# Column sums of the adaLN modulation: transposes and a VectorE reduction in place of products with ones, and a first group on one accumulator

## The chip, the cores and the metric

One core of a Trainium2 chip runs the kernel. The metric is device time in microseconds (us), lower is better; each time is that of one execution, and the time of a kernel is the median of its runs. One further execution is recorded by the hardware profiler, and all rows of the profile come from it.

## The reference

The reference is one decoder layer in f32 with T = 256 positions, D = 2048 channels and a feed-forward width of 5632. What matters here is the modulation: a vector c of 2048 numbers is multiplied by a matrix of 2048 x 12288, and the product's six segments shift and scale the two normalised inputs and gate the two sub-layers.

```python
mod = jax.nn.silu(c) @ w_ada[l] + b_ada[l]
shift1, scale1, gate1, shift2, scale2, gate2 = jnp.split(mod[:, None, :], N_MOD, axis=-1)
h = rms_norm(x, norm1_gain[l]) * (1 + scale1) + shift1
x = x + gate1 * mixing_sublayer(h, w_in[l], ...)
h = rms_norm(x, norm2_gain[l]) * (1 + scale2) + shift2
x = x + gate2 * swiglu(h, w_ffn_in[l], w_ffn_out[l])
```

The mixing sub-layer projects h by w_in (the combined in-projection), runs three token mixers (stick-breaking, dilated and gated linear attention), gates their outputs, adds them and projects by w_out.

## The kernel before, in words

**Products.** Every large product is made of three TensorE (PE) matmuls on operands that are split into a high and a low half. A weight tile is loaded by SyncE's DMA queue into `raw` (line 149, four buffers), ScalarE casts it to the high half `whi` (L163), VectorE (DVE) subtracts that from `raw` to get the low half `wlo` (L164), and then PE runs high x high (L171), low weight x high h (L172) and high weight x low h (L173), each 128x512. A buffer of `raw` comes free when the low half has been taken from it, so a load is issued on SP when DVE gets there.

**The modulation.** w_ada is not multiplied on PE. Each 128-row chunk of its columns is loaded (L335 for the stream, the `load` function for the first group), and DVE multiplies it by the matching 128 numbers of silu(c) and adds it into an accumulator (`ada_mac`, L296 and L298; tiles `ada` and `AR`). After sixteen chunks an accumulator holds 128 partial sums per column, one in each partition. They are added by PE: a product whose stationary operand is 128 columns of the accumulator and whose moving operand is one column of ones (`column_sum`, L355) gives the 128 sums as one column of PSUM. `finish_columns` adds the bias (L369) and, for a scale, forms (1 + scale) * gain (L372). `make_h` then writes the high half of h on ScalarE (L482), the f32 value on ScalarE (L488) or, in the first group, on DVE (L486), and the low half on DVE (L489).

**Order of the work.** The sixteen 128-row chunks of h and w_in are contracted in five groups, `GROUPS` = (0,2), (2,5), (5,8), (8,11), (11,16), each over sixteen column blocks of 512 (`proj_block`), whose sums are kept in SBUF between groups. Shift and scale of group 0 are made ahead of everything (`first_group`): there are fillers of PE called `keep_warm` (L470, products whose result is not used, in batches of 22, 13 and 14), the normalised input x transposed by PE (L462), the macs of 16 chunks in two accumulators (even and odd chunks), then 2 x 4 products with ones, where the sums over the even and the odd accumulator are accumulated in PSUM. Shift and scale of group g + 1 are made while group g is multiplied (`ada_stream`): groups 1 to 3 in one piece each, with three column sums for shift and three for scale, and group 4 in two pieces of five sums. `turn_piece` issues the sums three stream steps after the last mac (`ADA_LATE`), behind the latest matmul, and the finish at raised priority. Shift and scale of the second norm (`columns`, tiles `mod2`) are made in the background of later work, sixteen sums for each in four steps, with a finish behind each step.

The order on each engine is settled when the kernel is built, by the order of the program's text, by the priorities (`prio`) and by `issue_after`, which puts an instruction behind a named one. Each engine then runs its queue in order. In the profile six column sums are twelve rows of L355: an f32 product with ones appears as two rows.

## Time and profile before

| | before |
|---|---|
| runs | 1588.58, 1589.65, 1590.91 us |
| median | 1589.65 us |
| profiled execution | 1589.52 us, its span 1587.7 us |
| mean granted PE clock | 0.999 |
| PE busy | 1574.7 us, 99% of the span |
| DVE busy | 1329.8 us, 84% |
| ScalarE (ACT) busy | 932.4 us, 59% |
| DMA | 402.28 MB, mean 253 GB/s |

A timeline row reads: start in us, duration in us, engine, line, operation, output <- input, partitions x elements, and count, where equal neighbours are drawn together in one row; a bracket at the end tells how long the engine was idle before it and what ended that. Rows of a matmul overlap, so PE's pace is read from the distance of starts. `PEld` is the weight load of a matmul, which overlaps the matmul before it. In a table of windows the columns are the stretch, its length, the busy time and row count of PE, PEld, DVE, ACT and POOL, the granted PE clock (1.00 is full), the share of DMA and GB/s.

### The profile page before, as it was taken

The numbers are of one execution on the slowest core, as the hardware profiler recorded it, in microseconds if no ns is written. First come the engines' busy times: TensorE is split into PE (matmuls) and PEld (weight loads), VectorE is DVE, ScalarE is ACT, GpSimd is POOL, SyncE is SP. The second block draws the span as 40 slices with busy tenths as digits, with TensorE's granted clock in tenths as the row PEclk, the third lists the DMA queues.
The fourth block names the chain that finished last, engine by engine and source line by source line (L and its number), as shares of the span: only waits on it lengthen the run. The fifth ranks groups of instructions, "written<-read, shape, count | busy, mean of one in ns | idle before, by whom it ended". The sixth has DMA issues, their size and how long they took to land.

```text
span 1587.7 us, 20515 instructions
## 1 busy us (share of the span) xinstructions
PE 1574.7 (99%) x7263; PEld 1304.5 (82%) x7263; DVE 1329.8 (84%) x1628; ACT 932.4 (59%) x1355; POOL 12.3 (1%) x24
## 2 busy tenths in 40 slices
PE   8999999999999999999999999999999999999999
PEld 7888878888888888788888888888888888888887
DVE  6788876589897877879677887999999999999996
ACT  5777867987665463544444644555555555455553
POOL 1000000000000000000000000000000000000000
PEclk9999999999999999999999999999999999999999
DMA  9899989667788799899687786666666666976664
GB/s 333 302 331 301 318 300 307 209 212 236 222 306 280 252 326 318 296 323 327 228 273 235 266 296 208 212 195 195 202 204 201 198 199 208 307 239 192 219 210 150
DMA packets 196878, 402.28 MB, mean 253 GB/s; under 512 B 13662, under 2 KB 32772, under 8 KB 196776
## 3 DMA queue, kind: packets, MB, share of 16 engines
q1 hardware_dynamic: 195512, 397.75, 75.9%
q0 software_dynamic: 1088, 3.16, 0.6%
q8 instruction: 57, 0.93, 0.2%
q14 instruction: 45, 0.37, 0.1%
q10 hardware_dynamic: 176, 0.07, 0.0%
HBM read 395.68 MB, written 5.24 MB: 253 GB/s over the span
## 4 chain that ended last, share of the span: by engine, by line
PE 85%; DVE 5%; DMA 5%; ACT 3%; issue 2%; SPq 0%; DVEq 0%; ACTq 0%
PE acc L173 21%; PE acc L172 21%; PE acc L171 21%; PE misc L171 6%; PE misc L172 6%; PE misc L173 6%; DVE wlo L164 1%; DMA raw<-w_in 1%; ACT whi L163 1%; DVE wlo L1356 1%; PE misc L355 1%; DMA OS<-w_ada 1%; PE misc L832 1%; DMA raw<-w_ffn_in 1%; DMA OD<-w_ada 1%
## 5 line engine op out<-in xcount | busy, mean ns | idle before, releaser
L164 DVE TENSOR_TENSOR wlo<-raw,whi 128x1024 fp32r<-128x1024 f32 (+1 forms) x344 | 383.4, 1123 | 140.6 <-ACT whi L163 139.2
L163 ACT CAST whi<-raw 128x1024 fp32r<-128x1024 f32 (+1 forms) x344 | 332.9, 972 | 271.3 <-PE acc L173 163.1
L171 PE MATMUL acc<-whi,H 128*128 128x512 f32 x1145 | 449.1, 393 | 0.6 <-ACT whi L1370 0.3
L172 PE MATMUL acc<-wlo,H 128*128 128x512 f32 x1145 | 447.7, 391 | 0.6 <-DVE wlo L164 0.6
L173 PE MATMUL acc<-whi,H 128*128 128x512 f32 x1145 | 446.6, 391 | 0.6 <-DVE H L489 0.5
L172 PEld LDWEIGHTS acc<-wlo,H 128*128 128x128 f32 x1145 | 215.5, 188 | 46.5 <-DVE wlo L164 2.7
L173 PEld LDWEIGHTS acc<-whi,H 128*128 128x128 f32 x1145 | 215.2, 188 | 46.2 <-DVE H L489 1.3
L171 PEld LDWEIGHTS acc<-whi,H 128*128 128x128 f32 x1145 | 215.5, 188 | 44.6 <-ACT whi L1370 0.8
L1370 ACT CAST whi<-raw 128x1024 fp32r<-128x1024 f32 (+1 forms) x163 | 155.3, 968 | 110.7 <-PE acc L173 35.3
L1356 DVE TENSOR_TENSOR wlo<-raw,whi 128x1024 fp32r<-128x1024 f32 (+1 forms) x163 | 178.0, 1115 | 10.6 <-ACT whi L1370 9.5
L173 PE MATMUL acc<-whi,A 128*128 128x512 f32 x234 | 91.1, 389 | 0.0
L172 PE MATMUL acc<-wlo,A 128*128 128x512 f32 x224 | 87.4, 390 | 1.4 <-DVE wlo L164 1.4
L529 ACT COPY A<-acc 128x512 f32<-128x512 f32 x129 | 73.1, 584 | 25.9 <-PE acc L173 24.4
L171 PE MATMUL acc<-whi,A 128*128 128x512 f32 x224 | 87.4, 391 | 0.0
L171 PE MATMUL misc<-whi,H 128*128 128x512 f32 (+1 forms) x201 | 78.3, 389 | 0.2 <-DVE misc L1406 0.2
L172 PE MATMUL misc<-wlo,H 128*128 128x512 f32 (+1 forms) x201 | 78.0, 388 | 0.0
L173 PE MATMUL misc<-whi,H 128*128 128x512 f32 (+1 forms) x201 | 77.9, 387 | 0.0
L1370 ACT CAST A<-raw 128x1024 fp32r<-128x1024 f32 (+1 forms) x47 | 46.0, 988 | 34.4 <-PE acc L173 14.3
L1356 DVE TENSOR_TENSOR A<-raw,A 128x1024 fp32r<-128x1024 f32 (+2 forms) x59 | 61.3, 1050 | 5.5 <-ACT A L1370 5.0
L519 ACT COPY acc<-A 128x512 f32<-128x512 f32 x97 | 55.8, 597 | 3.8 <-DVE A L531 3.5
L298 DVE SCALAR_TENSOR_TENSOR ada<-AR,csil,ada 128x1024 f32<-128x1024 f32 x39 | 49.7, 1281 | 2.7 <-DMA AR<-w_ada 2.7
L173 PEld LDWEIGHTS acc<-whi,A 128*128 128x128 f32 x234 | 43.9, 188 | 9.1
(500 smaller groups left out, 2512.1 us busy)
## 6 DMA issues: line engine op xcount, KB each, us to landing
raw<-w_in SPq DMA_DIRECT2D x186, 512.0 KB, 4.9
raw<-w_ffn_in SPq DMA_DIRECT2D x176, 512.0 KB, 4.5
raw<-w_ffn_out SPq DMA_DIRECT2D x74, 512.0 KB, 5.1
AR<-w_ada SPq DMA_DIRECT2D x58, 512.0 KB, 5.0
raw<-w_in SPq DMA_DIRECT2D x64, 256.0 KB, 4.5
raw<-w_out SPq DMA_DIRECT2D x32, 512.0 KB, 5.0
KC<-w_ada SPq DMA_DIRECT2D x23, 512.0 KB, 5.9
KD<-w_ada SPq DMA_DIRECT2D x19, 512.0 KB, 5.9
```

What stands on the lines that cost most here:

```text
L163: state["cast"] = nc.scalar.copy(hi[:, :n, :], raw[:, :n, :])
L164: state["split"] = nc.vector.tensor_tensor(lo[:, :n, :], raw[:, :n, :], hi[:, :n, :].bitcast(F32), op=ALU.subtract)
L171: nc.tensor.matmul(ps, lh, rh, start=start, stop=False, skip_group_check=seeded)
L172: nc.tensor.matmul(ps, lh, rl, start=False, stop=False, skip_group_check=seeded)
L173: state["mm"] = nc.tensor.matmul(ps, ll, rh, start=False, stop=stop, skip_group_check=seeded)
L298: nc.vector.scalar_tensor_tensor(acc, raw, c, acc, op0=ALU.mult, op1=ALU.add)
L355: return nc.tensor.matmul(ps, acc, ones[:, 0:1], start=start, stop=stop)
L519: nc.scalar.copy(pss[t], A[b][:, t, :])
L529: nc.scalar.copy(A[b][:, t, :], pss[t])
L832: nc.tensor.matmul(ps[:n, t * N_GLA + h, :].rearrange("p (s l) -> p s l", l=L), at(f, h, t)[:, :n], odd(at(f, h, t)), start=True, stop=True,)
L1356: done = nc.vector.tensor_tensor(dst, x, y, op=ALU.subtract)
L1370: nc.scalar.copy(hi[:, :n, :], src)
```

## The change

There are three edits.

1. *First group.* One accumulator takes all sixteen macs, so each of the four sums is one product with ones. The third batch of fillers has seven matmuls for fourteen, and a new batch of two stands between the two pairs of sums. The first weight load is written out here; the low half of its two 128x512 parts is made in two instructions (in the new file L599), the first behind the last mac, the second behind the low half of h of chunk 0. Before, it was one instruction ahead of the last two macs.
2. *Stream and second norm.* `turned_sums` takes the place of the products with ones: for each 128 columns one PE transpose (with the identity as the moving operand) into a bank of PSUM, [128, n, 128], and then one DVE `reduce_sum` over the last axis for all n. In `turn_piece` n is 3, or 5 in two parts of 3 and 2; the reduction runs at raised priority and writes a small tile that the finish reads.
3. *Second norm.* For each segment there are four times four transposes and a reduction, and one finish over all sixteen columns behind them in place of four.

```diff
--- before.py
+++ after.py
@@ -37,7 +37,7 @@
 LOOK = 3
 DEFER = 4
 AHEAD = 4000
-WARM = (22, 13, 14)
+WARM = (22, 13, 7, 2)
 GROUPED = 16
 GROUPS = ((0, 2), (2, 5), (5, 8), (8, 11), (11, 16))
 ADA_BY = (16, 37, 58, 80)
@@ -289,13 +289,13 @@
 
     w_ada = I["w_ada"]
 
-    def ada_mac(acc, raw, k, zero=True, fresh=False):
+    def ada_mac(acc, raw, k, zero=True):
 
         c = csil[:, k : k + 1]
-        if k == 0 and zero or fresh:
-            nc.vector.tensor_scalar(acc, raw, c, None, op0=ALU.mult)
+        if k == 0 and zero:
+            return nc.vector.tensor_scalar(acc, raw, c, None, op0=ALU.mult)
         else:
-            nc.vector.scalar_tensor_tensor(acc, raw, c, acc, op0=ALU.mult, op1=ALU.add)
+            return nc.vector.scalar_tensor_tensor(acc, raw, c, acc, op0=ALU.mult, op1=ALU.add)
 
     ADA_TAGS = ("T4", "T5", "OS0", "OS1", "OS2", "OD")
     ADA_LATE = 3
@@ -347,20 +347,25 @@
     def turn_piece(g, js, acc, n):
         finish = mod_columns(g)
         for i, j in enumerate(js):
-            ps = column_sums(acc[:, i, :], n, state["mm"].ins)
+            sums = small([P, n])
+            half = (n + 1) // 2 if n > 4 else n
+            for a in range(0, n, half):
+                turned_sums(sums[:, a : min(n, a + half)], acc[:, i, a * P : min(n, a + half) * P], state["mm"].ins, True)
             with prio():
-                finish(j, ps)
-
-    def column_sum(ps, acc, start, stop):
-        return nc.tensor.matmul(ps, acc, ones[:, 0:1], start=start, stop=stop)
-
-    def column_sums(acc, n, behind):
-
-        ps = misc_bank([P, n])
+                finish(j, sums)
+
+    def column_sum(ps, acc):
+        return nc.tensor.matmul(ps, acc, ones[:, 0:1], start=True, stop=True)
+
+    def turned_sums(dst, acc, behind=None, soon=False):
+
+        n = dst.shape[1]
+        ps = misc_bank([P, n, P])
         for i in range(n):
-            with tc.issue_after(behind):
-                column_sum(ps[:, i : i + 1], acc[:, i * P : (i + 1) * P], True, True)
-        return ps
+            with tc.issue_after(behind) if behind is not None else nullcontext():
+                nc.tensor.transpose(ps[:, i, :], acc[:, i * P : (i + 1) * P], ident)
+        with prio() if soon else nullcontext():
+            nc.vector.reduce_sum(dst, ps, axis=AX.X)
 
     def finish_columns(ps, dst, seg, k0, gain_row=None):
 
@@ -565,29 +570,38 @@
         with tc.issue_after(state["row_turn"].ins):
             keep_warm(WARM[1])
         turned = norm1()
-        state["casts_after"] = turned[3].ins
-        early.extend(load_weights(w_in, 0, n, column(orders[0][0]), ahead=False))
-        split = state["split"]
+        c0 = column(orders[0][0])
+        raw = wp.tile([P, n, NB], F32, tag="raw", name=nm("raw"))
+        nc.sync.dma_start(raw, w_in[: n * P, c0 : c0 + NB].rearrange("(k p) c -> p k c", p=P))
+        hi, lo = (wp.tile([P, n, NB], F32R, tag=tag, name=nm(tag), bufs=4) for tag in ("whi", "wlo"))
+        with tc.issue_after(turned[3].ins):
+            nc.scalar.copy(hi, raw)
+        early.extend((hi[:, q, :], lo[:, q, :]) for q in range(n))
         load(range(5, KC // 2))
         with tc.issue_after(state["turn"].ins):
             keep_warm(WARM[2])
-        acc = S("ada", [P, 2, 2, w])
+        acc = S("ada", [P, 2, w])
         for k in range(KC):
-            with tc.issue_after(split.ins) if k >= 14 else nullcontext():
-                ada_mac(acc[:, k % 2], raws[k], k, fresh=k < 2)
+            done = ada_mac(acc, raws[k], k)
         sh, sc = mod1[:, 0, 0:n], mod1[:, 1, 0:n]
         chunk = lambda q: slice(q * P, (q + 1) * P)
         behind = state["warm"]
         for q in range(n):
             sums = misc_bank([P, 2])
             for j in range(2):
-                for i in range(2):
-                    with tc.issue_after(behind.ins):
-                        behind = column_sum(sums[:, j : j + 1], acc[:, i, j, chunk(q)], i == 0, i == 1)
-            with tc.issue_after(state["h_f"].ins) if q else nullcontext():
+                with tc.issue_after(behind.ins):
+                    behind = column_sum(sums[:, j : j + 1], acc[:, j, chunk(q)])
+            if q == 0:
+                with tc.issue_after(behind.ins):
+                    keep_warm(WARM[3])
+                behind = state["warm"]
+            with tc.issue_after(done.ins):
+                done = nc.vector.tensor_tensor(lo[:, q, :], raw[:, q, :], hi[:, q, :].bitcast(F32), op=ALU.subtract)
+            with tc.issue_after((state["h_f"] if q else done).ins):
                 finish_columns(sums[:, 0:1], sh[:, q : q + 1], SEG_SHIFT1, q)
                 finish_columns(sums[:, 1:2], sc[:, q : q + 1], SEG_SCALE1, q, ROW_N1)
             make_h(q, sh[:, q : q + 1], sc[:, q : q + 1], True)
+            done = state["h_lo"]
         gains[0] = (sh, sc)
 
     with prio(30000):
@@ -990,9 +1004,9 @@
             yield
         v = const.tile([P, KC], F32, name=nm("mod2"))
         for i in range(0, KC, 4):
-            ps = column_sums(acc[:, i * P : (i + 4) * P], 4, state["mm"].ins)
-            finish_columns(ps, v[:, i : i + 4], seg, i, ROW_N2 if seg == SEG_SCALE2 else None)
+            turned_sums(v[:, i : i + 4], acc[:, i * P : (i + 4) * P], state["mm"].ins)
             yield
+        finish_columns(v, v, seg, 0, ROW_N2 if seg == SEG_SCALE2 else None)
         mod2[seg] = v
 
     def rows_of(name, seg, acc):
```

PE at the end of the first group, before: the fillers (`acc` from `ones_r`), eight products with ones (`misc` from `ada`, four for each chunk of h) and the first matmuls of the first column block.

```order
L462 MATMUL misc_261<-H_41_214,A_13_109 128x128 x4
L470 MATMUL acc_282<-H_14_110,ones_r 128x512 x14
L355 MATMUL misc_314<-ones_r,ada_297 128x1 x4
L355 MATMUL misc_326<-ones_r,ada_297 128x1 x4
L171 MATMUL acc_341<-whi_269,H_15_112 128x512
L172 MATMUL acc_341<-wlo_270,H_15_112 128x512
L173 MATMUL acc_341<-whi_269,H_19_116 128x512
L171 MATMUL acc_342<-whi_269,H_15_112 128x512
L172 MATMUL acc_342<-wlo_270,H_15_112 128x512
```

The same place in the changed kernel:

```order
L467 MATMUL misc_261<-H_41_214,A_13_109 128x128 x4
L475 MATMUL acc_281<-H_14_110,ones_r 128x512 x7
L358 MATMUL misc_306<-ones_r,ada_289 128x1 x2
L475 MATMUL acc_309<-H_14_110,ones_r 128x512 x2
L358 MATMUL misc_320<-ones_r,ada_289 128x1 x2
L171 MATMUL acc_334<-whi_269,H_15_112 128x512
L172 MATMUL acc_334<-wlo_270,H_15_112 128x512
L173 MATMUL acc_334<-whi_269,H_19_116 128x512
L171 MATMUL acc_335<-whi_269,H_15_112 128x512
```

The fillers are seven, the sums two and two with two fillers between them, and the matmuls that follow are the same. Twelve matmuls on, where the first block of group 0 ends, the changed kernel has this on PE (`whi_359` and `whi_385` are the high halves of the second and third column block):

```order
L172 MATMUL acc_335<-wlo_270,H_15_112 128x512
L173 MATMUL acc_335<-whi_269,H_19_116 128x512
L171 MATMUL acc_355<-whi_359,H_15_112 128x512
L171 MATMUL acc_356<-whi_359,H_15_112 128x512
L171 MATMUL acc_381<-whi_385,H_15_112 128x512
L172 MATMUL acc_355<-wlo_360,H_15_112 128x512
L173 MATMUL acc_355<-whi_359,H_19_116 128x512
```

Three products with high halves, one of them of the third block, come ahead of the first that needs the second block's low half, `wlo_360`.

DVE at the end of the first group, before (`A` are the loaded chunks of w_ada, `wlo_270` the low half of the first weight tile, `mod` shift and scale, `H` out of `scr` the low half of h):

```order
L298 SCALAR_TENSOR_TENSOR ada_297<-A_54_276,csil,ada_297 128x512 x2
L164 TENSOR_TENSOR wlo_270<-raw_267,whi_269 128x1024
L298 SCALAR_TENSOR_TENSOR ada_297<-A_55_279,csil,ada_297 128x512 x2
L369 TENSOR_TENSOR mod_101<-misc_314,bada 128x1 x2
L372 SCALAR_TENSOR_TENSOR mod_101<-mod_101,vec 128x1
L486 TENSOR_SCALAR scr_322<-T_6_102,mod_101 128x256
L369 TENSOR_TENSOR mod_101<-misc_326,bada 128x1 x2
L372 SCALAR_TENSOR_TENSOR mod_101<-mod_101,vec 128x1
L489 TENSOR_TENSOR H_19_116<-scr_322,H_15_112 128x256
L486 TENSOR_SCALAR scr_334<-T_6_102,mod_101 128x256
L489 TENSOR_TENSOR H_19_116<-scr_334,H_15_112 128x256
```

And after:

```order
L298 SCALAR_TENSOR_TENSOR ada_289<-A_54_275,csil,ada_289 128x512 x2
L298 SCALAR_TENSOR_TENSOR ada_289<-A_55_278,csil,ada_289 128x512 x2
L599 TENSOR_TENSOR wlo_270<-raw_267,whi_269 128x512
L374 TENSOR_TENSOR mod_101<-misc_306,bada 128x1 x2
L377 SCALAR_TENSOR_TENSOR mod_101<-mod_101,vec 128x1
L491 TENSOR_SCALAR scr_316<-T_6_102,mod_101 128x256
L374 TENSOR_TENSOR mod_101<-misc_320,bada 128x1 x2
L377 SCALAR_TENSOR_TENSOR mod_101<-mod_101,vec 128x1
L494 TENSOR_TENSOR H_19_116<-scr_316,H_15_112 128x256
L599 TENSOR_TENSOR wlo_270<-raw_267,whi_269 128x512
L491 TENSOR_SCALAR scr_327<-T_6_102,mod_101 128x256
L494 TENSOR_TENSOR H_19_116<-scr_327,H_15_112 128x256
```

The low half left its place among the macs; its first part stands behind them and its second ahead of the last DVE steps of chunk 1.

DVE at the border from group 0 to group 1, before (`AR` is the accumulator of group 2's piece, `misc_729` and `misc_734` the sums of group 1's shift and scale):

```order
L296 TENSOR_SCALAR AR_176_772<-OS_177_773,csil 128x768
L369 TENSOR_TENSOR mod_101<-misc_729,bada 128x3
L369 TENSOR_TENSOR mod_101<-misc_734,bada 128x3
L164 TENSOR_TENSOR wlo_779<-raw_776,whi_778 128x1024
L372 SCALAR_TENSOR_TENSOR mod_101<-mod_101,vec 128x3
L298 SCALAR_TENSOR_TENSOR AR_176_772<-OD_809,csil,AR_176_772 128x768
L164 TENSOR_TENSOR wlo_785<-raw_782,whi_784 128x512
L298 SCALAR_TENSOR_TENSOR AR_176_772<-T_186_812,csil,AR_176_772 128x768
L489 TENSOR_TENSOR H_19_116<-scr_760,H_15_112 128x256
L489 TENSOR_TENSOR H_19_116<-scr_764,H_15_112 128x256
```

And after (`tiny` is the reduction's output):

```order
L296 TENSOR_SCALAR AR_179_769<-OS_180_770,csil 128x768
L368 TENSOR_REDUCE tiny_722<-misc_723 128x3
L368 TENSOR_REDUCE tiny_729<-misc_730 128x3
L374 TENSOR_TENSOR mod_101<-tiny_722,bada 128x3
L164 TENSOR_TENSOR wlo_776<-raw_773,whi_775 128x1024
L374 TENSOR_TENSOR mod_101<-tiny_729,bada 128x3
L164 TENSOR_TENSOR wlo_782<-raw_779,whi_781 128x512
L377 SCALAR_TENSOR_TENSOR mod_101<-mod_101,vec 128x3
L298 SCALAR_TENSOR_TENSOR AR_179_769<-OD_806,csil,AR_179_769 128x768
L298 SCALAR_TENSOR_TENSOR AR_179_769<-T_189_809,csil,AR_179_769 128x768
L494 TENSOR_TENSOR H_19_116<-scr_757,H_15_112 128x256
L164 TENSOR_TENSOR wlo_818<-raw_815,whi_817 128x1024
```

The two reductions and a 512-wide low half (`wlo_782`, in the place of `wlo_785`) now stand ahead of the gain's finish, and one multiply-add has left the place ahead of the first low half of h for the place behind the finish.

## The prediction, made before the changed kernel was run

> **What bounds the kernel now.** I read the page's busy times and its slices first, then the timeline at the places the diff touches.
>
> ```profile
> span 1587.7 us, 20515 instructions
> PE 1574.7 (99%) x7263; PEld 1304.5 (82%) x7263; DVE 1329.8 (84%) x1628; ACT 932.4 (59%) x1355; POOL 12.3 (1%) x24
> PE   8999999999999999999999999999999999999999
> DVE  6788876589897877879677887999999999999996
> PE 85%; DVE 5%; DMA 5%; ACT 3%; issue 2%; SPq 0%; DVEq 0%; ACTq 0%
> ```
>
> PE is 9 in every slice but the first, and the chain that ended last lies on PE for 85%. Since matmul rows overlap, busy time alone proves little; the starts do. A 128x512 matmul starts 0.23 us after the one before it (71.09 and 71.32 below) while its row reads 0.39. So wherever no larger gap shows, an instruction taken out of PE's stream shortens the run by the start-to-start time that it held. Three places matter: the first 33 us, the column sums within the stream, and the places where PE waits for DVE.
>
> **The sums in the stream.** Both of these timeline pieces have two 512-wide matmuls around an insert.
>
> ```profile
> 71.09 0.39 PE L172 MATMUL acc<-wlo,H 128*128 128x512 f32 x1
> 71.32 0.39 PE L173 MATMUL acc<-whi,H 128*128 128x512 f32 x1
> 71.55 1.39 PE L355 MATMUL misc<-ones_r,ada 128*128 128x1 f32 x12
> 72.80 0.49 PE L171 MATMUL acc<-whi,H 128*128 128x512 f32 x1
> ...
> 462.48 0.39 PE L173 MATMUL acc<-whi,H 128*128 128x512 f32 x1
> 462.71 1.47 PE L678 MATMUL misc<-ident,A 128*128 128x128 f32 x12
> 463.94 0.48 PE L171 MATMUL acc<-whi,H 128*128 128x512 f32 x1
> ```
>
> The program has six column sums at 71.55, and the trace has twelve rows: a product with ones takes two passes. It has twelve transposes at 462.71, and twelve rows: one pass each. The inserts hold PE for 71.32 to 72.80 less one start, 1.48 - 0.23 = 1.25 us, and 1.46 - 0.23 = 1.23 us. A pass costs 0.104 us in both; the transposes' 128 columns cost nothing extra beside the weight load. So each sum of 128 columns falls from two passes to one and saves 0.104 us.
>
> ```profile
> L355 PE MATMUL misc<-ones_r,ada x114: 164/250/250, 26.5 to 773.2; 128*128 128x1 f32 x114
> L355 PE MATMUL misc<-ones_r,AR x22: 164/250/250, 125.4 to 231.9; 128*128 128x1 f32 x22
> ```
>
> Of 114 + 22 = 136 rows 16 belong to the first group, which keeps the ones; 120 rows, 60 sums, are turned. Six of them (71.55) are at the border treated below. The other 54 give **-5.6 us** (54 x 0.104).
>
> **The first group.** Timeline of PE and DVE before the first real matmul:
>
> ```profile
> 20.46 3.02 DVE L298 SCALAR_TENSOR_TENSOR ada<-A,csil,ada 128x512 f32<-128x512 f32 x4 [1.36 <-DMA A<-w_ada]
> 23.19 3.51 PE L470 MATMUL acc<-H,ones_r 128*128 128x512 f32 x14
> 23.40 1.22 DVE L164 TENSOR_TENSOR wlo<-raw,whi 128x1024 fp32r<-128x1024 f32 x1
> 24.53 1.41 DVE L298 SCALAR_TENSOR_TENSOR ada<-A,csil,ada 128x512 f32<-128x512 f32 x2
> 26.54 1.84 PE L355 MATMUL misc<-ones_r,ada 128*128 128x1 f32 x16
> 27.52 0.22 DVE L369 TENSOR_TENSOR mod<-misc,bada 128x1 f32<-128x1 f32 x2 [1.58 <-PE misc L355]
> 28.69 0.50 PE L171 MATMUL acc<-whi,H 128*128 128x512 f32 x1 [0.31 <-ACT H L482]
> 29.60 0.43 DVE L489 TENSOR_TENSOR H<-scr,H 128x256 fp32r<-128x256 f32 x1
> 30.54 1.22 DVE L164 TENSOR_TENSOR wlo<-raw,whi 128x1024 fp32r<-128x1024 f32 x1
> ...
> 63.33 2.07 DVE L298 SCALAR_TENSOR_TENSOR ada<-OS,csil,ada 128x768 f32<-128x768 f32 x2
> ```
>
> ```profile
> L298 DVE SCALAR_TENSOR_TENSOR ada<-OS,csil,ada 128x768 f32<-128x768 f32 x16 | 16.2, 1013 | 0.3 <-DMA OS<-w_ada 0.3
> ...
> L298 DVE SCALAR_TENSOR_TENSOR ada<-A,csil,ada 128x512 f32<-128x512 f32 x14 | 10.4, 751 | 1.7 <-DMA A<-w_ada 1.7
> ```
>
> The last six multiply-adds run from 20.46 to 25.94, with the low half of 1.13 us of DVE between them. With that gone they follow one another, but with one accumulator each needs the last. The pair at 63.33, on one accumulator, takes 2.07 where one takes 1.013, so the second starts about 0.04 late. Six at 0.75 (751 ns) + 0.04 from 20.46 end at 25.15, 0.8 earlier; the first waited for its load, and the others' loads come every 0.75 as the back-to-back rows show. In before the sums started only at 26.54, since fourteen warm-up matmuls (23.19 + 3.51) stood ahead of them; seven end near 24.9. Given 0.05 for the signal and 0.19 for the weight load, the sums start at 25.4. The first finish (27.52) waited for eight passes of 1.84 / 16 = 0.115; now there are four, so it comes at 25.4 + 0.46 + 0.1 = 25.95. The first low part (0.69, by the 128x512 form below) runs from 25.15 to 25.84, hidden by these sums with 0.1 to spare. All that follows up to 28.69 is the same: **-1.55 us**.
>
> What is late next? The second low part stands ahead of the second low of h (29.60 to 30.03), which comes at 29.1 on the new clock, and of the next block's low half: 29.1 + 0.6 for a multiply-add + 1.2 = 30.8 or so. PE begins at 27.14, does twelve matmuls (to 30.2) and, in the new order, three products with high parts that need no low one (0.7): 30.9. No wait, but no slack either; if this fails, it costs some tenths. On SP the fifth weight load (24.65) is released by the early low half's end; it now comes near 28.2, and the loads behind it on SP's queue with it.
>
> ```profile
> 24.65 0.37 SPq L149 DMA_DIRECT2D raw<-w_in  x1
> ```
>
> ```profile
> DMA to landing us min/median/max: 10.0/10.0/10.0
> ```
>
> ```profile
> 26.50:29.90 3.40, 3.09 (x22) 2.64 (x21) 2.14 (x10) 1.63 (x3) 0.00 (x0) 1.00 1.05 380
> 29.90:33.30 3.40, 3.40 (x10) 2.62 (x9) 3.40 (x6) 2.04 (x3) 0.00 (x0) 0.50 1.08 360
> 33.30:36.70 3.40, 3.40 (x16) 2.80 (x16) 3.28 (x4) 2.78 (x4) 0.00 (x0) 0.99 0.99 347
> ```
>
> The DMA engines are full here (1.05) with loads issued earlier, and the load of 24.65 landed 10.0 us after issue, so 3.5 us of later issue are hidden by that backlog; without it they would be paid on a weight needed 10 us on.
>
> **The clock.** The same windows show granted clock 0.50 from 29.9 to 33.3: ten rows where 33.3 to 36.7 has sixteen. At half clock for 3.4 us PE loses about 1.6 us. In the stretch before it PE had 16 passes one column wide, a gap up to 28.69 and five matmuls. Now matmuls begin at 27.1, two warm-up ones lie between the sums, and that stretch would hold some eleven. I take it that the low grant goes: **-1.6 us**; bounds 0 and -1.7.
>
> [...]
>
> **The border of group 0 and 1.** The one sum whose result PE waits for:
>
> ```profile
> 73.05 1.23 DVE L164 TENSOR_TENSOR wlo<-raw,whi 128x1024 fp32r<-128x1024 f32 x1
> 74.20 0.16 DVE L372 SCALAR_TENSOR_TENSOR mod<-mod,vec 128x3 f32<-128x3 f32 x1
> 74.39 0.60 ACT L482 ACTIVATE H<-T,mod 128x256 fp32r<-128x256 f32 x1 [1.05 <-DVE mod L372]
> 75.20 0.69 DVE L164 TENSOR_TENSOR wlo<-raw,whi 128x512 fp32r<-128x512 f32 x1
> 76.73 0.76 DVE L489 TENSOR_TENSOR H<-scr,H 128x256 fp32r<-128x256 f32 x2
> 77.20 0.73 PE L173 MATMUL acc<-whi,H 128*128 128x512 f32 x2 [0.47 <-DVE H L489]
> ```
>
> ```profile
> L912 DVE TENSOR_REDUCE dmax<-T x12: 274/344/415, 475.8 to 483.3; 128x1 f32<-128x128 f32 x6, 128x1 f32<-128x256 f32 x6
> ```
>
> A reduction of 128 elements takes 0.28 us and one of 256 takes 0.41: 0.55 for 384 and 0.68 for 512, of which about 0.46 and 0.59 hold DVE when another follows (starts of 0.20 and 0.33 for the small ones, by the same step). Here two of 384, and in the new order also the 512-wide low half, come ahead of the gain's finish: from 72.0, two reductions end at 73.0, then the add, the low half (1.2), the second add and the 0.69: the finish stands at 75.0 instead of 74.20. ACT's high part of h then ends at 75.8, PE is there at 75.0 (0.63 earlier than now) and waits 0.8; the low of h comes at 77.5 for 76.8, and PE waits 0.7 again. Followed through the next forty matmuls this gives a net **+0.3** where cover would have given -0.63; bounds -0.6 and +1.3.
>
> At the last border (274) I find the high part of h 0.7 later, with eighteen matmuls ahead of its use: nothing. DVE gains eighteen reductions, 6 x 0.46 + 2 x (0.46 + 0.33) + 8 x 0.59 = 9.1 us, and loses nine small finishes. Those of 490 to 505 and 756 to 775 lie in slices with DVE at 7 and 6; PE waits there for nothing. In groups 1 to 3 cover is thinner:
>
> ```profile
>   DVE wlo L164: 2.6, 6
> ```
>
> ```profile
> 237.08 0.50 PE L172 MATMUL acc<-wlo,H 128*128 128x512 f32 x1 [0.41 <-DVE wlo L164]
> ```
>
> Between 200 and 260 us PE waits for a low half six times already, and the new order puts multiply-adds, which wait for loads, a place ahead of low halves. For reductions and order I take two more such waits: **+1.0**; bounds 0 and +4.3 (all ten reductions of the groups paid in full).
>
> **Sum**, against the profiled execution's 1589.52 us (span 1587.7 and 1.8 around it; the median is 0.13 higher): -5.6 - 1.55 - 1.6 + 0.3 + 1.0 = -7.45, or 1582.1; for the median 1582.2. Later stalls of PE (some near 630 and 1320) hang on loads issued from buffers that PE's own progress frees, so they move along.
>
> **Rivals.** [...] *DVE pays in part*: waits for low halves as at 237 at most borders, the last term at its +4.3: 1585.4, or 1587.0 without the clock's gain. For it: DVE at 84%; against: only 0.47 and 2.6 us of such waits in all of 30 to 300 us. *The transposes save nothing*, say since a turned accumulator meets a cost that the turned A at 462 did not: 1582.2 + 6.2 = 1588.4. Against: twelve rows in 1.23 us, with the same identity and the same kind of tile. *The slower side*: reductions are issued in DVE's one queue ahead of low halves that PE needs next; were all eighteen paid, 9.1 us, with the start's 1.55 and the 6.2 of passes but no clock gain, 1590.9. It decides once DVE's lead over PE at those places falls under the 0.46 to 0.59 of one reduction.
>
> **How the numbers follow.** Forecast 0.58; clock as it was 0.2; DVE in part 0.12; no saving 0.04; all reductions paid 0.06. Low end: no waits added and the border covered, -5.6 - 1.55 - 1.6 - 0.63 = -9.4, 1580.2, and some 0.4 for the spread of runs: 1579.8. High end: 1587.0. 0.2%, about what a measurement of this kernel can tell from no change, is 3.2 us: faster below 1586.5. The forecast, the clock's case and two thirds of DVE's: 0.86; the rest of that and the no-saving case 0.08; slower 0.06.
>
> **What would show it.** Right: the insert at 71 takes 0.65 us and those at 490 0.4; first real matmul near 27.1; clock 1.0 from 29.9; PE's wait before L173 of the second group about 1.5 in two parts. Wrong: a transpose pass over 0.12 us in the stream; PE waiting for low halves by more than 5 us in 30 to 300; a later 0.50 window.

## The result, and the profile after

Over nine runs each the changed kernel took a median of 1585.18 us (1583.89 to 1588.91) and the kernel before 1588.88 us (1586.16 to 1590.91). The ratio is 0.9982 with a 95% interval of 0.9972 to 0.9992: 2.9 us faster, between 1.3 and 4.4 (the two medians differ by 3.7). The forecast was 7.45 us. The time lies inside the range that was given (1579.8 to 1587.0), but only about two fifths of the forecast gain came.

The profiled execution took 1583.89 us, the fastest of the nine. Its page, span, busy times and chain:

```profile
span 1582.1 us, 20383 instructions
PE 1565.9 (99%) x7190; PEld 1293.5 (82%) x7190; DVE 1337.1 (85%) x1638; ACT 932.0 (59%) x1355; POOL 12.4 (1%) x24
PE 82%; DMA 7%; DVE 4%; ACT 3%; issue 2%; SPq 0%; ACTq 0%; DVEq 0%
```

DMA has 7% of the chain and had 5%: some work now waits for a load that it did not wait for. Where that is shows when one and the same matmul is looked up in both traces. The shift is its start after less its start before, so a falling column is time gained and a rising one time lost.

| matmul at, before | after | shift | what lies ahead of it |
|---|---|---|---|
| 28.69 | 26.47 | -2.22 | the first group |
| 69.70 | 66.59 | -3.11 | the half-clock window of before; a new wait at 30 us |
| 82.80 | 79.92 | -2.88 | border of groups 0 and 1 |
| 126.67 | 123.11 | -3.56 | sums of group 2 |
| 181.17 | 176.83 | -4.34 | sums of group 3 |
| 237.08 | 236.17 | **-0.90** | the rest of group 2's blocks, part of group 3's, sums of group 4's shift |
| 490.65 | 488.87 | -1.79 | sums of group 4's scale, first of the second norm |
| 773.30 | 768.23 | -5.07 | the other sums of the second norm |
| 1344.36 | 1338.72 | -5.64 | a wait of before near 1340 that the change does not touch |

The rows of the start and of the sums fall and the border's rises about as forecast. Between 181 and 237 us 3.4 us are given back. PE works there on the later part of group 2 and the first part of group 3, whose first matmul starts at 209.90 us before and at 208.58 after, while DVE makes the multiply-adds of group 4's shift and scale. Timeline of the changed kernel there, DVE, PE and SP's DMA issues:

```profile
201.22 0.42 SPq L337 DMA_DIRECT2D T<-w_ada  x1
...
202.06 0.88 DVE L298 SCALAR_TENSOR_TENSOR AR<-OS,csil,AR 128x640 f32<-128x640 f32 x1 [1.73 <-DMA OS<-w_ada]
...
202.86 0.55 DVE L296 TENSOR_SCALAR ada<-OS,csil 128x640 f32<-128x640 f32 x1
...
203.32 1.82 DVE L164 TENSOR_TENSOR wlo<-raw,whi 128x1024 fp32r<-128x1024 f32 x2
204.57 0.93 SPq L149 DMA_DIRECT2D raw<-w_in  x2
204.60 0.50 PE L172 MATMUL acc<-wlo,H 128*128 128x512 f32 x1 [1.04 <-DVE wlo L164]
```

Read it from the bottom: PE waits at 204.60 for a low half. DVE began that low half at 203.32, because a multiply-add stood ahead of it that had itself waited 1.73 us for its chunk of w_ada. And SP, which had issued nothing since 201.22, issues the next loads of w_in only at 204.57, when the low half has freed a buffer. One late load so delays the loads behind it. The low-half waits of the stretch from 180 to 240 us, from the profile's view of line 172, for before and for after:

```profile
  DVE wlo L164: 2.3, 5
```

```profile
  DVE wlo L164: 9.5, 11
```

These views add PE's own queue and its queue of weight loads, so they count about twice (so do the prediction's six waits between 200 and 260 us). By the starts alone (the distance from L171 to L172 less the usual 0.23) PE loses 1.15 us there before and 4.53 us after. The same sum is what "PE's wait" means below.

### The profile page after: what moved, and what is told of

Same layout as the page of the kernel before. It is cut to its first block, busy times and chain, and to the rows that moved or that the text cites. A ratio compares the mean times of both kernels' runs of the same rounds, so it can differ in the third digit from the quotient of the medians.

```text
span 1582.1 us, 20383 instructions
## 1 busy us (share of the span) xinstructions
PE 1565.9 (99%) x7190; PEld 1293.5 (82%) x7190; DVE 1337.1 (85%) x1638; ACT 932.0 (59%) x1355; POOL 12.4 (1%) x24
## 4 chain that ended last, share of the span: by engine, by line
PE 82%; DMA 7%; DVE 4%; ACT 3%; issue 2%; SPq 0%; ACTq 0%; DVEq 0%
PE acc L173 20%; PE acc L172 20%; PE acc L171 20%; PE misc L172 6%; PE misc L173 6%; PE misc L171 6%; DMA raw<-w_in 2%; DVE wlo L164 2%; DMA T<-w_ada 1%; DMA OS<-w_ada 1%; ACT whi L163 1%; DMA A<-w_ada 1%; DMA OD<-w_ada 1%; PE misc L846 1%; PE misc L1164 1%
## 5 line engine op out<-in xcount | busy, mean ns | idle before, releaser
L172 PE MATMUL acc<-wlo,H 128*128 128x512 f32 x1145 | 447.0, 391 | 3.4 <-DVE wlo L164 3.3
L171 PE MATMUL acc<-whi,H 128*128 128x512 f32 x1145 | 447.7, 392 | 1.6 <-ACT H L487 0.9
L172 PEld LDWEIGHTS acc<-wlo,H 128*128 128x128 f32 x1145 | 215.1, 188 | 50.0 <-DVE wlo L164 6.3
L171 PEld LDWEIGHTS acc<-whi,H 128*128 128x128 f32 x1145 | 215.0, 188 | 46.3 <-ACT H L487 1.4
L172 PE MATMUL acc<-wlo,A 128*128 128x512 f32 x224 | 87.5, 391 | 1.4 <-DVE wlo L164 1.3
L171 PE MATMUL acc<-whi,A 128*128 128x512 f32 x224 | 87.4, 391 | 0.0
L171 PE MATMUL misc<-whi,H 128*128 128x512 f32 (+1 forms) x201 | 78.2, 389 | 0.0
L172 PE MATMUL misc<-wlo,H 128*128 128x512 f32 (+1 forms) x201 | 78.0, 388 | 0.0
L1384 ACT CAST A<-raw 128x1024 fp32r<-128x1024 f32 (+1 forms) x47 | 46.0, 989 | 32.9 <-PE acc L173 12.4
L298 DVE SCALAR_TENSOR_TENSOR ada<-AR,csil,ada 128x1024 f32<-128x1024 f32 x39 | 49.6, 1281 | 3.6 <-DMA AR<-w_ada 3.6
```

Of the source, the lines that this page charges most:

```text
L171: nc.tensor.matmul(ps, lh, rh, start=start, stop=False, skip_group_check=seeded)
L172: nc.tensor.matmul(ps, lh, rl, start=False, stop=False, skip_group_check=seeded)
L298: return nc.vector.scalar_tensor_tensor(acc, raw, c, acc, op0=ALU.mult, op1=ALU.add)
L1384: nc.scalar.copy(hi[:, :n, :], src)
```

## The experiments

Thirteen kernels were run. The ratio is to the kernel before on the same chip. The next column counts, along DVE's rows in each trace, how many more multiply-adds stand ahead of a low half than before (mean over the 26 low halves that the kernel before makes from 185 to 241 us). The last two give PE's waits for low halves in us, each from one traced execution.

The expectations call the stretch from 180 to 240 us group 3. For kernels with the new first group their counts of multiply-adds are about 0.9 lower than the table's, as if its first low half, which is made there in two instructions, were counted twice.

| run | median us | ratio, 95% interval | multiply-adds ahead | wait 84 to 180 | wait 180 to 240 |
|---|---|---|---|---|---|
| before | - | 1 | 0 | 0.1 | 1.15 |
| after | 1585.18 | 0.9982 (0.9972 to 0.9992) | +1.8 | 0.2 | 4.53 |
| stream_ones | 1582.03 | 0.9962 (0.9949 to 0.9976) | -0.8 | 0.3 | 0.70 |
| mac_behind | 1581.13 | 0.9950 (0.9937 to 0.9964) | -3.0 | 0.2 | 1.54 |
| norm2_only | 1585.77 | 0.9979 (0.9970 to 0.9988) | 0 | 0.2 | 1.32 |
| stream_only | 1595.89 | 1.0042 (1.0029 to 1.0055) | +3.8 | 4.4 | 3.71 |
| ones_ahead | 1585.18 | 0.9978 (0.9968 to 0.9988) | +1.8 | 2.2 | 1.02 |
| border_ones | 1584.62 | 0.9969 (0.9957 to 0.9980) | +0.5 | 0.5 | 3.05 |
| first_only | 1587.44 | 0.9981 (0.9972 to 0.9990) | -0.8 | 0.3 | 0.62 |
| border_ones_mac_behind | 1581.90 | 0.9952 (0.9940 to 0.9965) | -2.6 | 0.5 | 0.69 |
| ones_level | 1584.75 | 0.9974 (0.9964 to 0.9984) | +0.5 | 1.3 | 0.90 |
| old_start_border_ones | 1589.52 | 1.0001 (0.9992 to 1.0011) | +1.0 | 0.2 | 2.64 |
| fillers_14 | 1584.71 | 0.9973 (0.9965 to 0.9982) | 0 | 0.2 | 2.82 |
| narrow_macs | 1584.92 | 0.9972 (0.9961 to 0.9983) | +1.8 | 0.2 | 3.96 |
| late_start | 1584.95 | 0.9968 (0.9955 to 0.9980) | +1.8 | 1.1 | 3.19 |

### stream_ones

The changed kernel's `turn_piece` with the old products:

```diff
-            turned_sums(sums[:, a : min(n, a + half)], acc[:, i, a * P : min(n, a + half) * P], state["mm"].ins, True)
+            ps = column_sums(acc[:, i, :], n, state["mm"].ins)
```

> The changed kernel with the 28 sums of the stream (groups 1 to 4) by products with ones again; the new first group and the transposes of the second norm stay. Three theories for the 4 us that PE newly waits for low halves between 180 and 240 us. Order: one more multiply-add stands ahead of a low half in VectorE's queue; in this kernel it is one to three fewer than before, so those waits fall under 1 us, and with 28 passes of 0.104 us back (+2.9) and the border's reductions gone (-0.9) the time is about 1583. Reductions: the same, since they are gone too. DMA: PE is as early as in the changed kernel and the loads come no earlier, so the waits stay at 3 to 4 us and the time is about 1587.

Measured: 1582.03 us, and PE waits 0.70 us. At the table's row of 181 us PE has a shift of -3.6 us against before (the changed kernel: -4.3), at the row of 237 us one of -4.2 (the changed kernel: -0.9). So an early PE does not have to pay such waits, and the DMA theory in that form falls. In the order that they bring with them, transposes in the stream cost more than they save: by the ratios the kernel with the products is 3.2 us faster, though the two intervals still overlap by 0.0004.

### mac_behind

```diff
-    with tc.issue_after(state["macs_after"]) if "macs_after" in state else nullcontext():
+    with tc.issue_after(state["macs_after"]) if "macs_after" in state else (tc.issue_after(state["split"].ins) if i in (3,) else nullcontext()):
```

> The changed kernel with the sixteen multiply-adds of group 4's shift put behind the latest low half that was written ahead of them, so that in the queue of VectorE 2 to 7 fewer stand ahead of a low half from 190 to 240 us; transposes, reductions and bytes are the same. Order: PE's waits for low halves between 185 and 240 us fall from about 4 us to under 1, the time is near 1582, unless group 4's sums come too late at the last border (then PE waits at 270 to 280). Reductions: the waits stay, 1585. DMA: the waits stay, 1585.

Measured: 1581.13 us, the lowest median of all, and PE's wait is 1.54 us for 4.53 with every transpose and reduction in place. What DVE's multiply-adds wait for between 180 and 240 us, from the profile's view of L298, in the changed kernel:

```profile
  DMA OS<-w_ada: 6.7, 6
  DMA T<-w_ada: 2.6, 2
  DMA OD<-w_ada: 0.5, 1
```

And in mac_behind:

```profile
  DMA OD<-w_ada: 3.0, 2
  DMA OS<-w_ada: 0.3, 1
```

9.8 us of waiting for w_ada at the head of DVE's queue have become 3.3. In place of it low halves now wait for ACT's high half, as this row of its timeline shows, which is the wait of an engine that has caught up:

```profile
199.26 1.23 DVE L164 TENSOR_TENSOR wlo<-raw,whi 128x1024 fp32r<-128x1024 f32 x1 [2.41 <-ACT whi L163]
```

### norm2_only and stream_only

The kernel before with `turned_sums` in `columns` alone, and in `turn_piece` alone:

```diff
-            ps = column_sums(acc[:, i * P : (i + 4) * P], 4, state["mm"].ins)
+            turned_sums(v[:, i : i + 4], acc[:, i * P : (i + 4) * P], state["mm"].ins)
```

```diff
-            ps = column_sums(acc[:, i, :], n, state["mm"].ins)
+            turned_sums(sums[:, a : min(n, a + half)], acc[:, i, a * P : min(n, a + half) * P], state["mm"].ins, True)
```

> The kernel before with the transposes for the second norm's 32 sums alone. All theories: each of the eight inserts at 490 to 505 and 755 to 773 us shortens by 0.42 us, VectorE's reductions there delay nothing, and the time is 3.3 us below the kernel before, about 1585.5.

> The kernel before with transposes and reductions for the stream's 28 sums alone. The order on VectorE comes out with 2 to 4 more multiply-adds ahead of a low half from group 2 on. Passes save 2.9 us, the border costs 0.9. Order: PE waits for low halves in groups 2 and 3 by more than the changed kernel's 4 us, so the time is 1591 or more. Reductions: the waits are those of the changed kernel, 4 us, 1590. DMA: PE is early by only 2 us here, the waits stay near 2 us at most, 1587 to 1588.

Measured: 1585.77 us, 3.05 below the kernel before's 1588.82 on that chip (15 runs); and 1595.89 us, 7.1 above it. The transposes of the second norm bring what their passes hold and no more is paid. Those of the stream, alone, make the kernel slower than any theory but the first had it. The order has nearly four more multiply-adds ahead, and the waits begin a group earlier. Its timeline near 160 us:

```profile
158.83 1.02 DVE L298 SCALAR_TENSOR_TENSOR ada<-OS,csil,ada 128x768 f32<-128x768 f32 x1 [2.59 <-DMA OS<-w_ada]
...
160.36 1.22 DVE L164 TENSOR_TENSOR wlo<-raw,whi 128x1024 fp32r<-128x1024 f32 x1
...
161.63 0.50 PE L172 MATMUL acc<-wlo,H 128*128 128x512 f32 x1 [1.10 <-DVE wlo L164]
```

It is the chain of 204.60 again: a load, a multiply-add, a low half, PE.

### ones_ahead, border_ones and ones_level

Is it the reductions after all? ones_ahead and ones_level are stream_ones with another pace of the stream, border_ones is the changed kernel with products for group 1:

```diff
-ADA_BY = (16, 37, 58, 80)
+ADA_BY = (16, 39, 60, 80)
```

```diff
+            if g == 1:
+                sums = column_sums(acc[:, i, :], n, state["mm"].ins)
...
+                continue
```

```diff
-ADA_BY = (16, 37, 58, 80)
+ADA_BY = (16, 38, 60, 80)
```

> The run stream_ones (products with ones in the stream) with the stream paced a little faster, two steps more by the ends of groups 1 and 2. VectorE's queue comes out with one multiply-add more ahead of a low half in groups 2 and 3 than the kernel before has, as in the changed kernel, but with no reduction in the stream. Order: PE waits for low halves between 180 and 240 us by 3 us or more and the time is 1585 to 1586. Reductions: nothing of the kind, the waits stay under 1 us as in stream_ones, 1582.

> The changed kernel with products with ones for the six sums of group 1 alone (the border from group 0 to 1); groups 2 to 4 keep 22 transposes with their reductions. VectorE's queue comes out with as many multiply-adds ahead of a low half as before the change, or one fewer. Order: the waits for low halves between 180 and 240 us fall from 4.5 us to about 1, the border's 0.9 goes, 0.6 of passes comes back, and the time is near 1581.5. Reductions: 22 of 28 sums still reduce ahead of low halves, the waits stay at 3 to 4 us, 1585.

> stream_ones (products with ones in the whole stream) paced so that in group 3 the same number of multiply-adds stands ahead of each low half as in border_ones, whose wait of 3 us between 180 and 240 us is not explained by one more multiply-add, since it has no more than the kernel before. Reductions explain it: here there are none, and the wait is under 1.2 us as in the kernel before. PE's lead explains it (PE comes 4 us earlier than before while the loads of w_ada that the multiply-adds wait for do not): the wait is 2.5 to 3.5 us here too. Time 1583 by the first, 1585 by the second; in groups 1 and 2 one multiply-add more may add up to 2 us in both.

Measured: ones_ahead lost 3.2 us against stream_ones (1585.18 for 1582.03; by the ratios 2.5, with intervals that overlap) with not one reduction in the stream. Its waits sum to 3.2 us from 84 to 240 us, where stream_ones has 1.0; they came mostly in group 1, and not after 180 us as was expected, although its order has 1.8 more multiply-adds ahead there. border_ones missed by 3 us: with half a multiply-add more ahead than before it waits 3.05 us and takes 1584.62. ones_level, with nearly the same places from 180 to 240 us and no reductions, waits 0.90 us there, 1.29 ahead of it and 1.15 behind it (two waits near 243 and 248), and its time is no better (1584.75). So reductions aren't needed for such waits, and the count of multiply-adds ahead does not by itself tell where they come.

### first_only and fillers_14

The new first group without any transposes, and stream_ones with `WARM = (22, 13, 14, 2)`.

> The changed kernel with all 60 sums of the stream and of the second norm by products with ones: the new first group alone. The start gives 1.8 (26.5 against 28.2 to 28.7 for the first real matmul), a new wait at 30 us takes 0.5, the low halves' waits are those of stream_ones. All theories: stream_ones plus 3.3 for the second norm, 1585.3; if the half-clock window in the profile of before was chance and rare, the sum from the kernel before is 1588.8 - 1.8 + 0.5 - 0.5 = 1587.

> stream_ones with fourteen fillers ahead of the first group's sums, as before, in place of seven. The multiply-adds end at 24.5 and the fillers near 26.1, so the first real matmul comes 1.4 us later than in stream_ones, near 27.9: the time is 1583.4 if PE's lead is worth itself, and 1582 if the lead of 1.4 us is taken back by waits for low halves anyway. All theories agree on the start; the lead theory expects the waits between 180 and 240 us to be no larger than in stream_ones.

Measured: first_only 1587.44 us, 2.1 below the kernel before's 1589.51 on that chip (21 runs; by the ratio 3.0, between 1.6 and 4.5), close to the second of the two numbers. fillers_14 starts its first real matmul at 27.77 (expected 27.9) and takes 1584.71; by the ratios that is 1.8 us more than stream_ones, with intervals that overlap, so neither of the two expected times is ruled out. Its order puts 0.8 multiply-adds more ahead of a low half than stream_ones, and PE waits 2.82 us for 0.70, with no reduction in the stream either.

One comparison here bounds what a single trace tells. From 60 to 240 us DVE, ACT and SP have the same rows in the same order in fillers_14, in before and in norm2_only, and PE is at the matmul of the table's 181 us row at 178.8, 181.2 and 179.1 us. Their waits from 180 to 240 us are 2.82, 1.15 and 1.32. So at one and the same order the wait of one execution can differ by 1.5 us from that of another.

### old_start_border_ones and border_ones_mac_behind

The kernel before with the transposes of groups 2 to 4 alone, and border_ones with mac_behind's edit.

> The kernel before with transposes and reductions for the 22 sums of groups 2 to 4 alone. PE keeps its old start, so it comes 1.3 to 2 us later at 180 us than in border_ones; in VectorE's queue 0 to 1 more multiply-adds stand ahead of a low half than before in group 2, 1 more in group 3. Passes save 2.3. Order alone: one more ahead, waits between 180 and 240 us of 3 to 4.5 us as in the changed kernel; 1589. Lead: with PE later the waits are 1.5 to 3 us, 1588. Reductions alone: waits of 3 to 4 us, as in border_ones.

> border_ones with the multiply-adds of group 4's shift behind the latest low half, as in mac_behind: 2 to 7 fewer ahead of a low half from 190 to 240 us. Order: little is left to gain there, 1581 to 1582, within 0.5 of border_ones. Reductions: waits as in mac_behind, 1580.8. If late sums of group 4 cost, PE waits at 270 to 290 us.

Measured: old_start_border_ones 1589.52 us, no change against before (ratio 0.9992 to 1.0011): the passes of 22 turned sums, 2.3 us, do not show in the time, and 1.5 us of them are found again in the wait, 2.64 us for 1.15. And border_ones_mac_behind 1581.90 us: in border_ones the multiply-adds placed behind take 2.7 us off the time and the wait from 180 to 240 us from 3.05 to 0.69. PE then waits 1.5 us near 244 for a low half that stands behind a multiply-add of group 4's scale, which itself waited 2.78 us for its load; it is not faster than mac_behind.

### narrow_macs and late_start

Two kernels that leave the changed kernel's order of multiply-adds and low halves as it is. The first lets half of group 4's multiply-adds take half of the columns, the second has eight fillers between the first group's pairs of sums.

```diff
+                        h = w // 2 if i in (3, 4) and k % 2 else w
-                        ada_mac(acc, raw, k)
+                        ada_mac(acc[:, :, :h], raw[:, :, :h], k)
```

```diff
-WARM = (22, 13, 7, 2)
+WARM = (22, 13, 7, 8)
```

> The changed kernel in which every second multiply-add of group 4's two pieces takes half of the columns (so half of group 4's shift and scale lacks every second chunk of w_ada). Every queue keeps its order, the loads and the reductions are the same; only sixteen multiply-adds shorten from 0.88 to about 0.48 us, 6 us of VectorE's time between 170 and 250 us. Capacity theory (in group 3 VectorE's work and its waits for w_ada fill the time, and what is over is paid by PE): PE's waits for low halves between 180 and 240 us fall from 4.5 to under 2 us, and the time to about 1582. Order alone (a multiply-add that waits for its load stands ahead of a low half): the load comes when it comes, the waits stay at 4 us or more, 1585.

> The changed kernel with eight fillers for two between the first group's two pairs of sums, so that PE starts its first block about 1 us later; VectorE's order of multiply-adds and low halves is that of the changed kernel. Capacity: the microsecond was taken back by the waits in group 3 anyway, so these shrink by 0.5 to 1 us and the time moves by less than 0.5 us, 1585 to 1585.7. Order alone: the waits stay at 4.5 us and the start is paid, 1586.2.

Measured: narrow_macs 1584.92 us and a wait of 3.96 us for 4.53; its short multiply-adds took 0.55 us and not 0.48. Its DVE was busy for 46.98 us between 180 and 240 us where the changed kernel's was for 50.14; what it gained it spent waiting for w_ada:

```profile
180.00:240.00 60.00, 56.97 (x247) 45.19 (x246) 46.98 (x70) 42.87 (x71) 0.00 (x0) 1.00 0.92 309
```

```profile
  DMA OS<-w_ada: 9.4, 7
  DMA OD<-w_ada: 1.5, 2
  DMA T<-w_ada: 0.8, 1
```

9.8 us of waiting have become 11.7, so the capacity theory falls: 3.2 us less work of DVE went with a wait of PE only 0.6 us shorter, and late_start, at the same order and with all of the work, waits 0.8 us less still. What sets the low halves' time there is the loads that the multiply-adds ahead of them wait for. late_start took 1584.95 us. The ratios of both lie below the changed kernel's, but the intervals of all three overlap, so the times alone do not tell them apart. In late_start's trace the first real matmul comes at 29.54 us, 3.1 later than in the changed kernel's (the six fillers more are 1.4 of it; the last multiply-add waited 1.15 us for its load, and part lies in a window at a granted clock of 0.50), and PE waits 3.19 us from 180 to 240 us and 1.06 ahead of that, 4.25 in all for 4.70. That a later start is given back by shorter waits is not shown.

## Why the prediction was wrong, point by point

**Passes: right.** Insert of four sums in the changed kernel:

```profile
488.51 0.60 PE L366 MATMUL misc<-ident,ada 128*128 128x128 f32 x4
488.87 0.47 PE L171 MATMUL acc<-whi,H 128*128 128x512 f32 x1
```

It holds PE for 0.36 us beyond a usual start; the eight rows of two passes at 489.85 in the trace of before held it for 0.81. All inserts outside the border together fell from 11.04 to 4.97 us, 6.1 for the 5.6 forecast, since a turned pass holds 0.09 to 0.096 us and not 0.104.

**Start: right.** The sums end the first group as the steps had it:

```profile
24.69 0.58 PE L358 MATMUL misc<-ones_r,ada 128*128 128x1 f32 x4 [0.25 <-DVE ada L298]
25.13 0.71 PE L475 MATMUL acc<-H,ones_r 128*128 128x512 f32 x2
25.31 0.22 DVE L374 TENSOR_TENSOR mod<-misc,bada 128x1 f32<-128x1 f32 x2 [0.16 <-PE misc L358]
...
26.47 0.50 PE L171 MATMUL acc<-whi,H 128*128 128x512 f32 x1 [0.29 <-ACT H L487]
```

The first real matmul came 2.22 us earlier; in this execution the fillers ahead already began 0.61 earlier (22.58 for 23.19), which leaves 1.6 for the 1.55 forecast. One thing there failed: "No wait, but no slack either" became a wait of 0.57 us, though not for the low half. The new order takes a product of the third block early as cover, and that one needs a bank of PSUM which ACT first has to copy out:

```profile
29.53 0.61 PE L171 MATMUL acc<-whi,H 128*128 128x512 f32 x2
30.55 0.50 PE L171 MATMUL acc<-whi,H 128*128 128x512 f32 x1 [0.41 <-ACT A L534]
```

**Clock: the first failed step.** "I take it that the low grant goes: -1.6." In the changed kernel's trace it is gone, but the runs do not show that the change took it away. The windows of first_only, which has the new first group, and of norm2_only, which has the old one:

```profile
28.86:32.27 3.41, 3.41 (x10) 2.63 (x9) 3.31 (x6) 2.37 (x3) 0.00 (x0) 0.50 1.04 361
```

```profile
28.06:31.47 3.41, 3.27 (x14) 2.44 (x15) 3.27 (x10) 3.17 (x6) 0.00 (x0) 1.00 1.06 382
```

Of fifteen traces three have a window at 0.50 there, before, first_only and late_start: one of the four with the old first group, two of the eleven with the new one. It comes and goes with the execution. So the step took one execution's chance for a term of the kernel. In both cases with the new first group the last multiply-add of that group had waited for its load (1.24 and 1.15 us); in the other nine it waited 0.04 us.

A part of the 1.6 us may still go with the change. The mean granted clock of every execution is on record: 0.99905 on average over 98 executions with the old first group, 0.99943 over 82 with the new one. Over 1588 us the difference is 0.6 us of PE's time, with a standard error of 0.2. The kernels and chips of the two sets are not the same, so this is not shown to come from the first group.

In before's trace the window begins 29.93 us into the span, in first_only's at 28.86, and in both the grant stays at 0.50 for 3.41 us. What sets its beginning the runs do not show.

**Border: right.** Reductions on DVE, of the changed kernel by form:

```profile
L368 DVE TENSOR_REDUCE mod<-misc 128x4 f32<-128x512 f32 x8 | 5.4, 688 | 0.9 <-PE misc L366 0.9
...
L368 DVE TENSOR_REDUCE tiny<-misc 128x3 f32<-128x384 f32 x8 | 4.2, 551 | 0.4 <-PE misc L366 0.4
```

0.55 and 0.69 us, as worked out (0.55 and 0.68). The gain's finish and what waits for it:

```profile
68.95 1.02 DVE L368 TENSOR_REDUCE tiny<-misc 128x3 f32<-128x384 f32 x2 [0.44 <-PE misc L366]
...
71.16 0.69 DVE L164 TENSOR_TENSOR wlo<-raw,whi 128x512 fp32r<-128x512 f32 x1
...
71.76 0.16 DVE L377 SCALAR_TENSOR_TENSOR mod<-mod,vec 128x3 f32<-128x3 f32 x1
...
72.61 0.50 PE L171 MATMUL acc<-whi,H 128*128 128x512 f32 x1 [0.63 <-ACT H L487]
```

PE's two waits, by the starts, are 0.79 and 0.65 us (0.8 and 0.7 forecast), and the border's net is -3.11 to -2.88, +0.23 for +0.3.

**Low halves: the second failed step, and the larger one.** "For reductions and order I take two more such waits: +1.0; bounds 0 and +4.3." The mechanism named in it was the right one ("multiply-adds, which wait for loads, a place ahead of low halves"), its size was not: PE's waits from 84 to 240 us rose from 1.25 to 4.70 us, +3.45, and from 185 to 241 us the order has not one but 1.8 multiply-adds more ahead of a low half. That these multiply-adds are the cause is shown by mac_behind, whose edit moves sixteen of them and nothing else, and whose interval lies wholly below the changed kernel's. The upper bound was reckoned from reductions, of whose work the runs show little: 3.2 us less work of DVE went with waits 0.6 us shorter (narrow_macs), no more than the scatter at one order, and waits of 3 us come without any reduction in the stream (ones_ahead, fillers_14); their own part was not measured apart. What the prediction left out is how long DVE in before already waits for w_ada between 180 and 240 us, from the profile's view of L298:

```profile
  DMA T<-w_ada: 5.0, 6
  DMA OD<-w_ada: 3.9, 3
  DMA OS<-w_ada: 2.4, 3
```

That is 11.3 us, so each place which a multiply-add moves ahead can hand one of these waits to PE. The rival *DVE pays in part* had nearly the time (1585.4), priced by the wrong instruction and with the clock's 1.6 us in it: its nearness is luck.

The account of the medians: -6.1 and the border's +0.2, the start's -1.6 and +0.6, the low halves' +3.45 make -3.4 us, or -4.0 with 0.6 for the clock; the measured ratio says -2.9 (1.3 to 4.4), so both fit. The profiled pair differs by 5.6 us: the trace of before also had the half-clock window (1.5 by the starts), its later fillers (0.6) and a wait near 1340 (0.6), and the trace of after none of these. With the -3.4 they would make 6.1, so 0.5 us is not accounted for.

The count of multiply-adds ahead sorts the orders by PE's waits, taken from 84 to 240 us (both columns of the table): 0.9 to 1.7 us with fewer ahead than before, 1.3, 1.5 and 3.0 with none more, 2.2 to 3.6 with 0.5 to 1.0 more, 3.2 to 4.7 with 1.8 more and 8.1 with 3.8 more. What stays open is the scatter at one order (fillers_14) and where along the stream a wait falls (ones_ahead), which neither reductions, nor DVE's work, nor PE's lead explains.

One thing does sort DVE's own waits. On SP the loads of w_ada move along with the multiply-adds from order to order, so that a multiply-add stays as close to its load as it was: from the issue of a load to its multiply-add the sixteen of group 4's shift have 5.6 to 6.2 us on average. By the view of L298 DVE waits 8.4 to 12.4 us for them from 180 to 240 us in every run but two. These are mac_behind and border_ones_mac_behind, where the multiply-adds move and the loads hardly do: there they have 14.6 and 11.6 us, and DVE waits 3.3 and 3.4 us.

## What to carry to other kernels

An edit that adds small instructions to a queue which a scheduler orders was priced here by the new order, not by their duration: look which instructions that wait for a load come to stand ahead of those that the busiest engine needs, and put them behind (mac_behind: PE's wait 1.54 us for 4.53). Transposes in place of products with ones were worth their passes where the queue had room (3 us in the second norm), and cost 3 us more than they saved where it had none. The kernel that keeps all of them and puts sixteen multiply-adds behind the low halves had the lowest ratio, 0.9950 (0.9937 to 0.9964); stream_ones (0.9962) is not told apart from it, and the products with ones together with these multiply-adds put behind were not run. A clock window seen in one trace is no term of a sum before a second trace shows it.

## What the runs showed of the hardware

A product with one column of ones takes two passes of 0.101 to 0.104 us, and a transpose of 128 columns one of 0.09 to 0.096, so the 128 columns that it moves cost no more here than the one. The granted clock had a window at 0.50 about 28 to 30 us into three of fifteen executions (from 29.93 us for 3.41 in before, from 28.86 for 3.41 in first_only), in a stretch where PE went from one-column passes to matmuls, and in executions of the same first group it had none (1.00 in norm2_only from 28.06 to 31.47 us, in the changed kernel from 28 to 34).
